# A threshold search on whole float32 scores, with a third tile counted by signs on ScalarE

## Chip, cores and metric

One core of one Trainium2 chip. The metric is the device time of one execution of the whole program in microseconds (us); the time before is the median of 3 runs.

## The reference, cut to what matters

The program is one step of a two-layer encoder trunk for 1024 prompt tokens and 32 sample tokens. The second layer's mixer is sparse attention: an indexer gives every query a score for every key, and each query attends to the 256 keys with the highest scores.

```
def dsa_attend_block(q, qi, wi, qpos, k, v, ki, kpos, topk):
    ...
    logits = jnp.einsum('bthd,bsd->bths', qi.astype(jnp.float32), ki.astype(jnp.float32)) * (IDX_DIM ** -0.5)
    score = jnp.einsum('bths,bth->bts', jax.nn.relu(logits), wi.astype(jnp.float32) * (IDX_HEADS ** -0.5))
    allowed = (kpos[None, :] // CHUNK) <= (qpos[:, None] // CHUNK)
    score = jnp.where(allowed[None], score, NEG)
    vals, idx = lax.top_k(score, topk)
    ...
```

## The kernel before, in words

The program runs in stages: the state-space layer, a feed-forward layer, the index scores, the projections of keys, values and queries, the attention, its output projection, and a second feed-forward layer. Residual and activations stay in SBUF; matrix products are made from exact high and low parts, three matmuls for each.

Tokens stand in nine tiles: 0 to 7 are 128 prompt tokens each, 8 is the sample's 32. Tile t may see `ext[t]` keys: 128 (t + 1) for the prompt, 1056 for the sample. Tiles 2 to 8 choose among more than 256 keys, and `index_scores` leaves their float32 scores in `sc[t]`, one row per query.

`select` (line 1063) finds the 256th highest score of each row, bit by bit, for all rows of all seven tiles at once. A step sets one bit of the candidate threshold, counts each row's scores that reach it, and keeps the bit where there are at least 256. VectorE counts tiles 7, 5, 4, 3 and 2 (`COMPS`) by a comparison with an accumulated output (line 1099); ScalarE counts tiles 8 and 6 (`SIGNS`) by the accumulated sign of score minus threshold (line 1102). Line 1105 compares the counts with 256 for all tiles (`up`), line 1111 sets the bit (`key`), line 1108 makes the next candidate, which both engines wait for. These three work on 2 to 7 columns; all such values lie in one tile, `small`.

The sign tiles are searched over whole float32 scores. The comparison tiles are searched over 16-bit halves: line 1080 copies the upper halves out as bfloat16 (`half`), 15 steps search those, then lines 1133 to 1141 count the scores above the found upper half and replace `half` by the lower halves of the scores that share it, and 16 steps search those as unsigned integers, with two more small operations in a step (lines 1146 and 1151).

The search is a generator. `project_heads` computes the projections in six jobs (keys, four groups of queries, values) of nine token tiles. A tile's product takes 24 matmuls (lines 772 to 774) into a PSUM bank, six of them in turn; ScalarE copies it out (line 1217) and after each copy `beside` lets 0.6 of a step of the search be recorded (`RATE`), on ScalarE behind that copy. So 54 copies and 31 steps share the engines, in the order in which a scheduler puts them on each queue; every queue is run in order. For keys and queries, three tiles at a time, ScalarE squares (line 1238), VectorE sums (line 1244), and GpSimd scales and rotates (lines 1247, 812 to 815, 1274). GpSimd also splits the weights (lines 140, 141).

`attend` follows. It takes the PSUM banks over once all copies are done, and reads keys, values and queries back from DRAM. `make_mask` turns a tile's threshold into a mask one step of `attend` ahead of its use: VectorE counts the scores above the threshold (line 1176); for a sign tile the key may be one too low, so three small operations raise it (lines 1181 to 1183) and line 1176 runs a second time; then lines 1185 to 1189 on VectorE and 1190, 1191 on GpSimd write the mask. On GpSimd's queue the split of the next queries (lines 1202, 1203) stands behind them, and PE's transposes of these (line 1336) wait for it.

Of the kernel before, what the change touches and what calls it, by code (L numbers as in the profile page):

```python
# [40 lines left out]
SIGNS, COMPS = [8, 6], [7, 5, 4, 3, 2]  # L41
# [8 lines left out]
class Trunk:  # L50
    """Shared tiles and helpers; the residual lives in xt[feature % 128, feature // 128, token]."""
# [13 lines left out]
    def open_dense(self, ctx):  # L65
        """The residual, from the first mixer's recurrence on."""
        self.main = ctx.enter_context(self.tc.tile_pool(name="main", bufs=1, reuse_waits="tile"))
        self.xt = self.main.tile([P, KD, T], F32, name="xt")

    def open_tables(self, ctx):  # L70
        """Constants of the second mixer."""
        nc, I = self.nc, self.I
        pool = ctx.enter_context(self.tc.tile_pool(name="tab", bufs=1, side="right", reuse_waits="tile"))
        self.tab = {}
        for nm in ("cos", "sin"):
            self.tab[nm] = pool.tile([P, 9, 16], F32, name=nm)
            nc.scalar.dma_start(self.tab[nm], I["c_" + nm])
# [17 lines left out]
    def load_vectors(self, pool):  # L95
        """Per-feature vectors, one column of 128 features each."""
# [34 lines left out]
    def weight(self, view, pool=False):  # L131
        """view [128, n] (rows on partitions): its two exact parts, as stationary operands; pool: split by the Pool engine."""
# [14 lines left out]
    def weight_rows(self, view, sh):  # L147
        """weight of a view whose rows lie apart."""
# [10 lines left out]
    def product(self, ps, terms):  # L159
        """ps += sum over (wh, wl, xh, xl) of w^T x, in float32 accuracy."""  # L160
# [8 lines left out]
    def rsqrt(self, y, m, tmp, iters=3):  # L169
        """y = m ** -0.5 elementwise; tmp: like y."""  # L170
# [68 lines left out]
    def store_block(self, pool, b):  # L239
        """y rows of block b."""  # L240
# [14 lines left out]
    def exp(self, pool, dst, x):  # L255
        """dst = exp(x) to float32 accuracy (range reduction, polynomial, exponent bits)."""
# [19 lines left out]
    def cmul(self, pool, orr, oi, xr, xi, yr, yi):  # L276
        """(orr + i oi) = (xr + i xi)(yr + i yi); shapes [.., s, n] already broadcast alike."""
# [44 lines left out]
    def ssm_params(self, pool, tmp, ld):  # L322
        """State-major tables of the discretized recurrence: partition = (re n | im n). The norm's gain is part of the inputs' taps."""
# [19 lines left out]
        # th = 2 pi k + (r + rl)  # L343
# [21 lines left out]
        # powers a^0 .. a^8  # L365
# [6 lines left out]
        # f = (a - 1) / lambda  # L372
# [22 lines left out]
        # rows to be transposed: 0-7 (Re af | Re af), 8-15 (-Im af | Im af), 16-23 (Re a | Re a),  # L395
        # 24-31 (-Im a | -Im a), 32 |a|^8, 33 state
# [24 lines left out]
        # turns per chunk of 8 tokens, in three parts  # L421
# [16 lines left out]
        # stationary rows (group | group): [0] parts 0 and 1, less a small shift; [1] part 0; [2] parts 1 and 2  # L438
# [13 lines left out]
        # input and output maps, state-major  # L452
# [63 lines left out]
        # the sample's rows take the place of b, c and the powers, which are of no more use  # L516
# [13 lines left out]
    def ssm(self):  # L530
        """xh + xl = gelu(S5(rmsnorm(x))), feature k*128 + g*16 + q at [q*8 + g, k]."""
        nc, I, O = self.nc, self.I, self.O
        C = 133  # chunk columns: 128 of the prompt, the sample's start state, 4 of the sample
        with ExitStack() as ctx:
# [34 lines left out]
            G0 = (0, 3, 6)  # groups are worked on three at a time  # L569
# [3 lines left out]
            def taps(o):  # L573
                """Input taps a^(7-j) f B, output taps C a^d, and |a|^8 of 8 groups."""
# [23 lines left out]
            def maps(o, d):  # L598
                """Within-chunk operands: inputs to state (re | im | re), inputs to outputs."""
# [25 lines left out]
            def angles(o, s):  # L625
                """cos and sin of the state's turns up to each chunk; the groups' inputs, [(j, cin), chunk]."""
# [31 lines left out]
            def states(d, w):  # L658
                """The states at the chunks' ends, turned back: the scan needs |a|^8 only; then their turned parts."""
# [38 lines left out]
            def rows(o):  # L698
                """Feature-major rows, gelu, parts in token order."""
# [34 lines left out]
            # final states  # L734
# [30 lines left out]
    def project(self, ps, t, w, kw, a, b):  # L765
        """ps[token, column] = xn[tokens of tile t] @ W[:, a:b], w: the parts of W's rows in pieces of kw k-tiles."""
# [9 lines left out]
    def open_spares(self):  # L776
        """Small tiles of the second mixer's first part, in the rooms of the norm's tiles."""
# [31 lines left out]
    def rotary(self, eng, r, x, cos, sin):  # L809
        """x[..., 0:16] rotated in place; cos, sin: tables broadcast to x[..., 0:16]; r: scratch like x[..., 0:16]."""  # L810
# [6 lines left out]
    def split_rows(self, hi, lo, ps):  # L817
        """Parts of ps: hi (all rows), lo."""
# [4 lines left out]
    def stack(self, dst, ps):  # L823
        """ps rows (x; x) -> dst rows (high part of x; low part of x)."""
# [4 lines left out]
    def attn_inputs(self, ctx):  # L829
        """Selection masks (in ctx's pool), and the projected heads, written to DRAM."""  # L830
# [18 lines left out]
        # the masks take the place of the scores  # L849
        mask = {i: sc[i].bitcast(BF)[:, : ext[i]] for i in sc}  # L850
        self.mask = mask
        with ExitStack() as pctx:
# [19 lines left out]
            def beside(ins):  # L872
                """Steps of the search, behind a copy of the projections."""
# [11 lines left out]
    def index_scores(self, ip, W, OQI, OKI, cos, sin, sc):  # L885
        """sc[i][q, key] = index scores of the query tiles that choose among more than 256 keys."""
# [11 lines left out]
        def keys(t, ps):  # L898
            """Keys of tile t rotated; returns the rest of the work."""
# [17 lines left out]
        def queries(t, ps, h0):  # L917
            """Four heads' queries of tile t rotated; returns the rest of the work."""
# [37 lines left out]
        # heads 4-7 with the keys and the weights of the heads, then heads 0-3  # L956
# [18 lines left out]
        # the sample: a sum over the heads by a product with their weights, four heads of the 32 queries and a fourth of  # L975
        # the keys (256 of the cache, 8 of its own) at a time; rows of the sum: (fourth, query)
# [3 lines left out]
        def sample_weights():  # L980
            """Weights as (head, query) x query, zeros around."""
# [79 lines left out]
    def select(self, mp, wk, sc):  # L1061
        """Thresholds: the 256th highest score of each row, bit by bit; make_mask does the rest. Scores that are counted by
        comparisons are searched by their upper, then by their lower halves, the others (counted by signs) as a whole."""
        nc = self.nc
        ext = self.ext
        BF, U16 = mybir.dt.bfloat16, mybir.dt.uint16
# [5 lines left out]
        rooms = [[wk.tile([P, T], F32, tag="kh", name="half").bitcast(BF), 2 * T]]  # L1072
        for tag in ("q", "q", "qi", "qi"):
            rooms.append([wk.tile([P, 512], F32, tag=tag, name="half", bufs=2).bitcast(BF), 1024])
        half = {}
        for t in sorted(COMPS, key=lambda t: -ext[t]):
            room = next(r for r in rooms if r[1] >= ext[t])
            room[1] -= ext[t]
            half[t] = room[0][: rows(t), room[1] : room[1] + ext[t]]
# [4 lines left out]
        sm = mp.tile([P, 13, n], F32, name="small")  # L1084
        d = {}
        for i, nm in enumerate(("cnt", "need", "thr", "a", "b", "low", "try", "key", "m", "cand", "up", "val", "x")):
            d[nm] = sm[:, i] if i < 7 else sm[:, i].bitcast(I32)
        cut = lambda v, i: v[: rows(ts[i]), i : i + 1]
        sg, cm = lambda v: v[:, 0:ns], lambda v: v[:, ns:n]
# [4 lines left out]
        def count(x, xs, op=ALU.is_ge, signs=None):  # L1094
            for i, t in enumerate(ts):
                o = cut(d["cnt"], i)
                if i >= ns:
                    turn[0] ^= 1
                    nc.vector.tensor_scalar(
                        junk[turn[0]][: rows(t), : ext[t]], xs[t], x if x == 0.0 else cut(x, i), 0.0, op0=op, op1=ALU.add, accum_out=o)  # L1100
                elif signs is not None:
                    nc.scalar.activation(junk[2][: rows(t), : ext[t]], sc[t][: rows(t)], AF.Sign, bias=signs if signs == 0.0 else cut(signs, i), accum_out=o)

        def reached():
            nc.vector.tensor_tensor(d["up"], d["cnt"], d["thr"], op=ALU.is_ge)

        def candidate(f, bit):
# [35 lines left out]
        for bit in range(15, -1, -1):  # L1143
            if ns:
                candidate(sg, bit)
# [584 lines left out]
```

## Time and profile before

| | us |
|---|---|
| median of 3 runs (lowest, highest) | 2805.51 (2801.63, 2806.05) |
| span of the profiled execution | 2799.6 |
| the median over that span | 5.9 |
| PE busy | 2582.2 (92%) |
| VectorE (DVE) busy | 1640.5 (59%) |
| ScalarE (ACT) busy | 976.6 (35%) |
| GpSimd (POOL) busy | 448.1 (16%) |

The profile gives one execution, taken by the hardware profiler; its time outside the span isn't given, so the span is its own time. PE's share is 92% over the whole, but the 40 slices of the profile dip for PE in the slices from 1390 us on, and VectorE's rise to nearly full: a stage with another limit. Times of rows are from the span's start.

### The profile page before, as it was taken

How to read it: one execution, taken by the hardware profiler on the slowest of the kernel's cores; microseconds unless marked ns; L12 is line 12 of the kernel's file. 1: busy time of each engine (PE TensorE's matmuls, PEld its weight loads, DVE VectorE, ACT ScalarE, POOL GpSimd, SP SyncE). 2: the span in 40 equal slices, each digit the busy share in tenths (PEclk: the TensorE clock that was granted, in tenths of full speed). 3: DMA queues.
4: the chain of work that ended last, by engine and by line, in shares of the span. 5: the costliest groups of instructions: out<-in, count | busy, mean ns of one | idle time of the engine just before them, and what ended most of it. 6: DMA issues, size and time to landing. Idle time of an engine off the chain costs nothing. (4 is left out here: it accounts for less than half of the span.)

```text
span 2799.6 us, 43287 instructions
## 1 busy us (share of the span) xinstructions
PE 2582.2 (92%) x17203; PEld 2473.0 (88%) x17203; DVE 1640.5 (59%) x3487; ACT 976.6 (35%) x1947; POOL 448.1 (16%) x696
## 2 busy tenths in 40 slices
PE   2887999999999999997986689999999999999999
PEld 2676999999999999996886667778999999999998
DVE  8886225644444444478799977663554444444443
ACT  4565213311111111134544466773331111111112
POOL 4672001100000000012144243220110000000000
PEclk9998999999999999998998889999999999999999
DMA  4334211111111111110121211212111111111111
GB/s 94 60 59 109 80 46 46 46 46 46 46 46 46 46 46 46 46 37 14 48 66 47 69 40 25 52 27 69 46 46 46 46 46 46 46 46 46 46 38 63
DMA packets 220662, 140.29 MB, mean 50 GB/s; under 512 B 50429, under 2 KB 212261, under 8 KB 220461
## 3 DMA queue, kind: packets, MB, share of 16 engines
q1 hardware_dynamic: 216733, 130.90, 17.0%
q10 hardware_dynamic: 3728, 6.64, 0.7%
q8 instruction: 135, 2.21, 0.3%
q14 instruction: 66, 0.54, 0.1%
HBM read 112.68 MB, written 13.40 MB: 45 GB/s over the span
## 5 line engine op out<-in xcount | busy, mean ns | idle before, releaser
L164 PE MATMUL ps_mm<-xh,whi 128*128 128x352 f32 x2688 | 870.4, 324 | 5.0 <-ACT whi L143 5.0
L166 PE MATMUL ps_mm<-xh,wlo 128*128 128x352 f32 x2688 | 869.6, 324 | 0.0
L165 PE MATMUL ps_mm<-xl,whi 128*128 128x352 f32 x2688 | 868.6, 323 | 0.0
L164 PEld LDWEIGHTS ps_mm<-xh,whi 128*128 128x128 f32 x2688 | 506.5, 188 | 5.3 <-ACT whi L143 5.2
L165 PEld LDWEIGHTS ps_mm<-xl,whi 128*128 128x128 f32 x2688 | 506.3, 188 | 0.0
L166 PEld LDWEIGHTS ps_mm<-xh,wlo 128*128 128x128 f32 x2688 | 506.0, 188 | 0.2 <-DVE wlo L144 0.2
L144 DVE TENSOR_TENSOR wlo<-wraw,whi 128x1024 fp32r<-128x1024 f32 (+1 forms) x145 | 175.5, 1222 | 416.4 <-ACT whi L143 416.4
L143 ACT CAST whi<-wraw 128x1024 fp32r<-128x1024 f32 (+1 forms) x145 | 149.9, 1047 | 712.1 <-PE ps_mm L165 702.3
L1603 DVE TENSOR_TENSOR xt<-xt,ps_mm 128x352 f32<-128x352 f32 x528 | 269.4, 520 | 191.5 <-PE ps_mm L166 191.4
L164 PE MATMUL ps_mm<-hh,whi 128*128 128x352 f32 x1056 | 341.0, 323 | 1.5 <-DVE xt L1603 1.5
L165 PE MATMUL ps_mm<-hl,whi 128*128 128x352 f32 x1056 | 340.9, 323 | 0.0
L166 PE MATMUL ps_mm<-hh,wlo 128*128 128x352 f32 x1056 | 340.7, 323 | 0.0
L1584 POOL COPY tails<-a 128x2 f32<-128x2 f32 x44 | 39.8, 904 | 1229.5 <-ACT a L1573 1229.5
L772 PE MATMUL ps_mm<-whi,xh 128*128 128x256 f32 (+3 forms) x560 | 165.8, 297 | 42.5 <-ACT raw L1217 42.5
L164 PEld LDWEIGHTS ps_mm<-hh,whi 128*128 128x128 f32 x1056 | 198.4, 188 | 2.1 <-DVE xt L1603 2.0
L166 PEld LDWEIGHTS ps_mm<-hh,wlo 128*128 128x128 f32 x1056 | 198.4, 188 | 0.0
L165 PEld LDWEIGHTS ps_mm<-hl,whi 128*128 128x128 f32 x1056 | 198.4, 188 | 0.0
L1591 DVE TENSOR_TENSOR c<-c,ps_mm 128x352 f32<-128x352 f32 (+2 forms) x176 | 71.5, 428 | 159.2 <-PE ps_mm L166 112.6
L774 PE MATMUL ps_mm<-whi,xl 128*128 128x256 f32 (+3 forms) x560 | 163.6, 293 | 0.0
L773 PE MATMUL ps_mm<-wlo,xh 128*128 128x256 f32 (+3 forms) x560 | 163.6, 293 | 0.0
L772 PEld LDWEIGHTS ps_mm<-whi,xh 128*128 128x128 f32 (+1 forms) x560 | 106.4, 190 | 47.4 <-ACT raw L1217 41.2
L1573 ACT COPY a<-ps_mm 128x352 f32<-128x352 f32 (+2 forms) x176 | 61.9, 378 | 242.1 <-PE ps_mm L166 242.0
(420 smaller groups left out, 3992.4 us busy)
## 6 DMA issues: line engine op xcount, KB each, us to landing
wraw<-in_ffn_w_up_dram SPq DMA_DIRECT2D x88, 512.0 KB
wraw<-in_ffn_w_down_dram SPq DMA_DIRECT2D x44, 512.0 KB
wraw<-in_ssm_w_glu_dram SPq DMA_DIRECT2D x128, 64.0 KB
wraw<-in_attn_w_in_dram SPq DMA_DIRECT2D x14, 512.0 KB
zo<-yo SPq DMA_DIRECT2D x64, 66.5 KB
xcm<-in_x_prompt_dram SPq DMA_DIRECT2D x8, 512.0 KB
cps<-cp SPq DMA_DIRECT2D x16, 256.0 KB
xrow<-in_x_prompt_dram ACTq DMA_DIRECT2D x8, 512.0 KB
```

The lines of the kernel that those rows point to most:

```text
L143: nc.scalar.copy(hi, raw)
L144: nc.vector.tensor_sub(lo, raw, hi.bitcast(F32))
L164: nc.tensor.matmul(ps, wh, xh, start=(i == 0), stop=False)
L165: nc.tensor.matmul(ps, wh, xl, start=False, stop=False)
L166: nc.tensor.matmul(ps, wl, xh, start=False, stop=(i == n - 1))
L772: self.nc.tensor.matmul(ps, xh, hi[:, c, a:b], start=(k == 0), stop=False)
L773: self.nc.tensor.matmul(ps, xh, lo[:, c, a:b], start=False, stop=False)
L774: self.nc.tensor.matmul(ps, xl, hi[:, c, a:b], start=False, stop=(k == KD - 1))
L1573: nc.scalar.copy(u["a"][:, co + 2 : co + 2 + n], ps[:, to - b * BLK : to - b * BLK + n])
L1584: nc.gpsimd.tensor_copy(tails[:, u["f"], 0:2], u["a"][:, TP : TP + 2])
L1591: nc.vector.tensor_mul(h, h, bv[:, to - b * BLK : to - b * BLK + n])
L1603: nc.vector.tensor_add(self.xt[:, m, blocks[b]], self.xt[:, m, blocks[b]], ps[:, :BLK])
```

## The change

All seven tiles are searched over whole float32 scores, in 31 alike steps (bits 30 to 0) after the first count. The copies of halves, the passage from upper to lower halves and the small operations of the lower steps are gone. Tile 2 moves from the comparisons to the signs, so VectorE counts four tiles a step and ScalarE three. (The change also drops comments, so the lines behind them have smaller numbers: line 1102 becomes 1089, 1099 becomes 1092, 1105 becomes 1093, 1111 becomes 1105, 1108 becomes 1103, 1217 becomes 1169, 1176 becomes 1128, 1190 becomes 1142, 1202 becomes 1154.)

```diff
-SIGNS, COMPS = [8, 6], [7, 5, 4, 3, 2]
+SIGNS, COMPS = [8, 6, 2], [7, 5, 4, 3]
...
-        half = {}
-        for t in sorted(COMPS, key=lambda t: -ext[t]):
...
-            nc.vector.tensor_copy(half[t], sc[t].bitcast(BF)[: rows(t), 1 : 2 * ext[t] : 2])
-        y = {t: half[t].bitcast(U16) for t in half}
...
-        def count(x, xs, op=ALU.is_ge, signs=None):
+        def count(x):
             for i, t in enumerate(ts):
-                o = cut(d["cnt"], i)
-                if i >= ns:
+                o, v = cut(d["cnt"], i), sc[t][: rows(t)]
+                c = x if x == 0.0 else cut(x, i)
+                if i < ns:
+                    nc.scalar.activation(junk[2][: rows(t), : ext[t]], v, AF.Sign, bias=c, accum_out=o)
+                else:
                     turn[0] ^= 1
-                    nc.vector.tensor_scalar(
-                        junk[turn[0]][: rows(t), : ext[t]], xs[t], x if x == 0.0 else cut(x, i), 0.0, op0=op, op1=ALU.add, accum_out=o)
...
+                    nc.vector.tensor_scalar(junk[turn[0]][: rows(t), : ext[t]], v, c, 0.0, op0=ALU.is_ge, op1=ALU.add, accum_out=o)
             nc.vector.tensor_tensor(d["up"], d["cnt"], d["thr"], op=ALU.is_ge)
...
-        for bit in range(30, 15, -1):
-            candidate(all_, bit)
-            count(cf, half, signs=cf)
-            reached()
-            settle(all_, bit)
-            yield
...
-        count(cf, half, ALU.is_gt)
...
-                nc.vector.tensor_scalar(half[t], half[t], cut(cf, i), cut(d["a"], i), op0=ALU.is_equal, op1=ALU.mult)
...
-        for bit in range(15, -1, -1):
...
-            nc.vector.tensor_scalar_add(cm(d["try"]), cm(d["low"]), float(1 << bit))
-            count(d["try"], y, signs=cf)
...
-            nc.vector.scalar_tensor_tensor(cm(d["low"]), cm(d["up"]), float(1 << bit), cm(d["low"]), op0=ALU.mult, op1=ALU.add)
+        for bit in range(30, -1, -1):
+            nc.vector.scalar_tensor_tensor(d["cand"], d["key"], 1 << bit, d["x"], op0=ALU.bitwise_or, op1=ALU.bitwise_xor)
+            count(d["cand"].bitcast(F32))
+            nc.vector.scalar_tensor_tensor(d["key"], d["up"], bit, d["key"], op0=ALU.logical_shift_left, op1=ALU.bitwise_or)
             if bit:
                 yield
```

VectorE at the last step of the search before and after (line 1099, now 1092, counts a tile; `small` holds the columns). Before:

```order
L1099 TENSOR_SCALAR junk,small<-half,small 128x1024
L1099 TENSOR_SCALAR junk,small<-half,small 128x768
L1099 TENSOR_SCALAR junk,small<-half,small 128x640
L1099 TENSOR_SCALAR junk,small<-half,small 128x512
L1099 TENSOR_SCALAR junk,small<-half,small 128x384
L1105 TENSOR_TENSOR small<-small 128x7
L1111 SCALAR_TENSOR_TENSOR small<-small 128x2
L1151 SCALAR_TENSOR_TENSOR small<-small 128x5
L1108 SCALAR_TENSOR_TENSOR small<-small 128x2
L1146 TENSOR_SCALAR small<-small 128x5
```

After:

```order
L1092 TENSOR_SCALAR junk,small<-score_11145,small 128x1024
L1092 TENSOR_SCALAR junk,small<-score_11143,small 128x768
L1092 TENSOR_SCALAR junk,small<-score_11142,small 128x640
L1092 TENSOR_SCALAR junk,small<-score_11141,small 128x512
L1093 TENSOR_TENSOR small<-small 128x7
L1105 SCALAR_TENSOR_TENSOR small<-small 128x7
L1103 SCALAR_TENSOR_TENSOR small<-small 128x7
```

A count and two small operations are gone, and the counts read the scores themselves.

ScalarE at the end of the projections, where the last step's signs stand among the last copies of values (`raw`) and their stores to DRAM (`vd`); `score_11146` is tile 8, `score_11144` tile 6, `score_11140` tile 2. Before:

```order
L1102 ACTIVATE junk,small<-score_11146,small 32x1056
L1102 ACTIVATE junk,small<-score_11144,small 128x896
L1217 COPY raw<-ps_mm 128x256
L1224 DMA vd<-raw 128x3x256
L1224 DMA out_v_prompt_dram<-raw 128x3x256
L1217 COPY raw<-ps_mm 128x256 x2
```

After:

```order
L1089 ACTIVATE junk,small<-score_11146,small 32x1056
L1089 ACTIVATE junk,small<-score_11144,small 128x896
L1169 COPY raw<-ps_mm 128x256
L1089 ACTIVATE junk,small<-score_11140,small 128x384
L1176 DMA vd<-raw 128x3x256
L1176 DMA out_v_prompt_dram<-raw 128x3x256
L1169 COPY raw<-ps_mm 128x256 x2
```

A third sign pass stands behind the other two, ahead of the last stores and copies; a copy can come between two passes.

GpSimd at the start of the attention, with tile 2's mask (`ms`, written to the place of `score_11140`) and the splits of queries (`qp`). Before:

```order
L1202 TENSOR_SCALAR qp<-qr 128x4x64
L1203 TENSOR_TENSOR qp<-qr,qp 128x4x64
L1190 TENSOR_TENSOR ms<-ms 128x384
L1191 TENSOR_SCALAR score_11140<-ms 128x384
L1202 TENSOR_SCALAR qp<-qr 128x4x64
L1203 TENSOR_TENSOR qp<-qr,qp 128x4x64
```

After:

```order
L1154 TENSOR_SCALAR qp<-qr 128x4x64
L1155 TENSOR_TENSOR qp<-qr,qp 128x4x64
L1142 TENSOR_TENSOR ms<-ms 128x384
L1154 TENSOR_SCALAR qp<-qr 128x4x64
L1143 TENSOR_SCALAR score_11140<-ms 128x384
L1155 TENSOR_TENSOR qp<-qr,qp 128x4x64
```

The second split still ends behind both operations of the mask.

## Rows read from the trace of the kernel before

**Rows 1.** Stretches of time: length, busy PE, PEld, DVE, ACT, POOL, clock, DMA.

```profile
1390.00:1604.00 214.00, 161.52 (x1279) 155.84 (x1278) 207.85 (x546) 102.10 (x199) 84.80 (x103) 0.91 0.17 53
```

**Rows 2.** Waits of 1390 to 1640 us: total us, times, longest.

```profile
PE ps_mm L772 <- ACT raw L1217: 42.5, 17, 13.0
...
PE ps_t L1324 <- ACT raw L1217: 9.0, 1, 9.0
```

**Rows 3.** DVE timeline, an upper step: start, us, engine, line, operation, [idle before].

```profile
1481.99 1.28 DVE L1099 TENSOR_SCALAR_CACHE_REDUCE junk<-half,small 128x1024 bf16<-128x1024 bf16 x1
...
1485.59 0.61 DVE L1099 TENSOR_SCALAR_CACHE_REDUCE junk<-half,small 128x384 bf16<-128x384 bf16 x1
1486.13 0.08 DVE L1099 DVE_READ_ACCUMULATOR junk<-half,small 128x1 f32 x1
1486.32 0.17 DVE L1105 TENSOR_TENSOR small<-small 128x7 int32<-128x7 f32 x1
1486.70 0.17 DVE L1111 SCALAR_TENSOR_TENSOR small<-small 128x7 int32<-128x7 int32 x1 [0.22 <-DVE small L1105]
...
1487.11 1.28 DVE L1099 TENSOR_SCALAR_CACHE_REDUCE junk<-half,small 128x1024 bf16<-128x1024 bf16 x1
```

**Rows 4.** DVE timeline, the passage between the halves.

```profile
1491.25 0.95 DVE L1244 TENSOR_REDUCE room<-sq 128x12 f32<-128x768 f32 x1
...
1493.01 0.17 DVE L1111 SCALAR_TENSOR_TENSOR small<-small 128x7 int32<-128x7 int32 x1
...
1509.46 1.27 DVE L1099 TENSOR_SCALAR_CACHE_REDUCE junk<-half,small 128x1024 bf16<-128x1024 uint16 x1
...
1510.66 0.61 DVE L1141 SCALAR_TENSOR_TENSOR half<-score,small,half 128x384 uint16<-128x384 uint16 x1
```

**Rows 5.** DVE timeline, a lower step, from its first count to the next one's.

```profile
1515.66 1.28 DVE L1099 TENSOR_SCALAR_CACHE_REDUCE junk<-half,small 128x1024 bf16<-128x1024 uint16 x1
...
1520.66 1.28 DVE L1099 TENSOR_SCALAR_CACHE_REDUCE junk<-half,small 128x1024 bf16<-128x1024 uint16 x1
```

**Rows 6.** DVE timeline, the last copy of halves, ahead of the first count.

```profile
1392.99 0.69 DVE L1080 COPY half<-score 128x1024 bf16<-128x1024 bf16 x1 [0.24 <-POOL score L1059]
```

**Rows 7.** Groups by shape: busy us, mean ns, idle before; search and masks.

```profile
L1099 DVE TENSOR_SCALAR_CACHE_REDUCE junk<-half,small 128x1024 bf16<-128x1024 bf16 x16 | 20.4, 1278 | 0.5
...
L1176 DVE TENSOR_SCALAR_CACHE_REDUCE ms<-score,small 128x1024 bf16<-128x1024 f32 x1 | 1.3, 1273 | 0.0
```

**Rows 8.** Groups by shape, the sign passes on ScalarE.

```profile
L1102 ACT ACTIVATE junk<-score,small 32x1056 bf16<-32x1056 f32 x31 | 36.4, 1176 | 107.3 <-DVE small L1108 79.5 <-DVE small L1146 27.8
L1102 ACT ACTIVATE junk<-score,small 128x896 bf16<-128x896 f32 x31 | 32.1, 1037 | 0.6
```

**Rows 9.** ACT timeline, a step's sign passes and copies, and a square.

```profile
1482.05 1.18 ACT L1102 ACTIVATE junk<-score,small 32x1056 bf16<-32x1056 f32 x1 [2.32 <-DVE small L1108]
...
1483.35 1.04 ACT L1102 ACTIVATE junk<-score,small 128x896 bf16<-128x896 f32 x1
...
1484.39 0.63 ACT L1217 COPY raw<-ps_mm 128x256 f32<-128x256 f32 x2
...
1488.34 0.83 ACT L1238 ACTIVATE sq<-raw 128x768 f32<-128x768 f32 x1
```

**Rows 10.** Timelines of DVE, POOL and PE, tile 2's mask.

```profile
1616.11 0.62 DVE L1189 SCALAR_TENSOR_TENSOR ms<-ms,small 128x384 bf16<-128x384 f32 x1
...
1616.86 0.91 POOL L1190 TENSOR_TENSOR ms<-ms 128x384 bf16<-128x384 bf16 x1 [6.52 <-ACT p L1362]
...
1619.72 0.75 PE L1336 MATMUL ps_t<-identr,qp 128*128 128x128 f32 x4 [4.21 <-POOL qp L1203]
```

**Rows 11.** DVE timeline, the raising of a sign tile's key (tile 6).

```profile
1670.97 0.14 DVE L1181 TENSOR_SCALAR small<-small 128x1 int32<-128x1 f32 x1
...
1672.34 1.15 DVE L1176 TENSOR_SCALAR_CACHE_REDUCE ms<-score,small 128x896 bf16<-128x896 f32 x1
```

**Rows 12.** Groups of the search's stretch, DVE: busy us, mean ns.

```profile
L1108 DVE SCALAR_TENSOR_TENSOR small<-small 128x2 int32<-128x2 int32 (+1 forms) x31 | 11.2, 360 | 0.4
```

More of the change, by code (lines that the diff above doesn't have):

```diff
@@ L1065, in select @@
         ext = self.ext
-        BF, U16 = mybir.dt.bfloat16, mybir.dt.uint16
+        BF = mybir.dt.bfloat16
         K = 256.0
@@ L1071, in select @@
         rows = lambda t: self.toks[t][1]
-        rooms = [[wk.tile([P, T], F32, tag="kh", name="half").bitcast(BF), 2 * T]]
-        for tag in ("q", "q", "qi", "qi"):
-            rooms.append([wk.tile([P, 512], F32, tag=tag, name="half", bufs=2).bitcast(BF), 1024])
-        half = {}
-        for t in sorted(COMPS, key=lambda t: -ext[t]):
-            room = next(r for r in rooms if r[1] >= ext[t])
-            room[1] -= ext[t]
-            half[t] = room[0][: rows(t), room[1] : room[1] + ext[t]]
-            nc.vector.tensor_copy(half[t], sc[t].bitcast(BF)[: rows(t), 1 : 2 * ext[t] : 2])
-        y = {t: half[t].bitcast(U16) for t in half}
         junk = [wk.tile([P, T], BF, tag="r", name="junk", bufs=3) for _ in range(3)]
         turn = [0]
-        sm = mp.tile([P, 13, n], F32, name="small")
+        sm = mp.tile([P, 9, n], F32, name="small")
         d = {}
-        for i, nm in enumerate(("cnt", "need", "thr", "a", "b", "low", "try", "key", "m", "cand", "up", "val", "x")):
-            d[nm] = sm[:, i] if i < 7 else sm[:, i].bitcast(I32)
+        for i, nm in enumerate(("cnt", "need", "thr", "key", "m", "cand", "up", "val", "x")):
+            d[nm] = sm[:, i] if i < 3 else sm[:, i].bitcast(I32)
         cut = lambda v, i: v[: rows(ts[i]), i : i + 1]
-        sg, cm = lambda v: v[:, 0:ns], lambda v: v[:, ns:n]
         nc.vector.memset(d["cnt"], 0.0)
@@ L1092, in select @@
             nc.vector.memset(d["thr"][:, i : i + 1], 2 * K - ext[t] if i < ns else K)
-        def count(x, xs, op=ALU.is_ge, signs=None):
+        def count(x):
             for i, t in enumerate(ts):
-                o = cut(d["cnt"], i)
-                if i >= ns:
-                    turn[0] ^= 1
-                    nc.vector.tensor_scalar(
-                        junk[turn[0]][: rows(t), : ext[t]], xs[t], x if x == 0.0 else cut(x, i), 0.0, op0=op, op1=ALU.add, accum_out=o)
-                elif signs is not None:
-                    nc.scalar.activation(junk[2][: rows(t), : ext[t]], sc[t][: rows(t)], AF.Sign, bias=signs if signs == 0.0 else cut(signs, i), accum_out=o)
-        def reached():
-            nc.vector.tensor_tensor(d["up"], d["cnt"], d["thr"], op=ALU.is_ge)
-        def candidate(f, bit):
-            nc.vector.scalar_tensor_tensor(f(d["cand"]), f(d["key"]), 1 << bit, f(d["x"]), op0=ALU.bitwise_or, op1=ALU.bitwise_xor)
-        def settle(f, bit):
-            nc.vector.scalar_tensor_tensor(f(d["key"]), f(d["up"]), bit, f(d["key"]), op0=ALU.logical_shift_left, op1=ALU.bitwise_or)
-        all_ = lambda v: v
-        count(0.0, half, signs=0.0)
-        reached()
+                o, v = cut(d["cnt"], i), sc[t][: rows(t)]
[3 more added lines that the diff above has]
+                else:
+                    turn[0] ^= 1
+                    nc.vector.tensor_scalar(junk[turn[0]][: rows(t), : ext[t]], v, c, 0.0, op0=ALU.is_ge, op1=ALU.add, accum_out=o)
+            nc.vector.tensor_tensor(d["up"], d["cnt"], d["thr"], op=ALU.is_ge)
+        count(0.0)
         nc.vector.tensor_single_scalar(d["key"], d["up"], 31, op=ALU.logical_shift_left)
@@ L1118, in select @@
         nc.vector.tensor_single_scalar(d["m"], d["m"], TOP, op=ALU.bitwise_or)
+        nc.vector.tensor_copy(d["x"], d["m"])
         if ns:
-            nc.vector.tensor_single_scalar(sg(d["x"]), sg(d["m"]), TOP, op=ALU.bitwise_xor)
-        nc.vector.tensor_copy(cm(d["x"]), cm(d["m"]))
-        nc.vector.tensor_scalar(d["a"], d["up"], 2.0, -1.0, op0=ALU.mult, op1=ALU.add)
-        nc.vector.tensor_scalar(d["b"], d["up"], 65535.0, -65535.0, op0=ALU.mult, op1=ALU.add)
-        cf = d["cand"].bitcast(F32)
@@ L1126, in select @@
-        for bit in range(30, 15, -1):
-            candidate(all_, bit)
-            count(cf, half, signs=cf)
-            reached()
-            settle(all_, bit)
-            yield
-        nc.vector.tensor_tensor(cm(d["cand"]), cm(d["key"]), cm(d["m"]), op=ALU.bitwise_xor)
-        nc.vector.tensor_single_scalar(cm(d["cand"]), cm(d["cand"]), -65536, op=ALU.bitwise_and)
-        count(cf, half, ALU.is_gt)
-        nc.vector.tensor_scalar(cm(d["thr"]), cm(d["cnt"]), -1.0, K, op0=ALU.mult, op1=ALU.add)
@@ L1137, in select @@
-        nc.vector.memset(d["low"], 0.0)
-        for i, t in enumerate(ts):
-            if i >= ns:
-                nc.vector.tensor_scalar(half[t], half[t], cut(cf, i), cut(d["a"], i), op0=ALU.is_equal, op1=ALU.mult)
-                nc.vector.scalar_tensor_tensor(
-                    y[t], sc[t].bitcast(U16)[: rows(t), 0 : 2 * ext[t] : 2], cut(d["b"], i), half[t], op0=ALU.add, op1=ALU.mult)
-        for bit in range(15, -1, -1):
-            if ns:
-                candidate(sg, bit)
-            nc.vector.tensor_scalar_add(cm(d["try"]), cm(d["low"]), float(1 << bit))
-            count(d["try"], y, signs=cf)
-            reached()
-            if ns:
-                settle(sg, bit)
-            nc.vector.scalar_tensor_tensor(cm(d["low"]), cm(d["up"]), float(1 << bit), cm(d["low"]), op0=ALU.mult, op1=ALU.add)
+            nc.vector.tensor_single_scalar(d["x"][:, 0:ns], d["m"][:, 0:ns], TOP, op=ALU.bitwise_xor)
```

2 lines of the change are left out of this document (removed).

## The prediction

> **What bounds the kernel now.** Over the whole program PE is the busiest, so the view to read first is the one of busy time by stretches, to see whether the change lies where PE is the limit. It doesn't. In the 214 us of the projections, in which the search runs, VectorE is busy 207.85 us, PE 161.52, ScalarE 102.10, GpSimd 84.80 [rows 1]. Next, the waits of that stretch, to see who is held up by whom: PE waits 42.5 us in 17 places for ScalarE's copies out of PSUM, and then 9.0 us, at the change to the attention, for the last of them [rows 2]. Those copies are not slow; they stand in ScalarE's queue behind sign passes, and the sign passes wait 107.3 us for the next candidate from VectorE, at line 1108 in the upper and the lower steps and at line 1146, which the queue puts last in a lower step [rows 8]. So the chain is: VectorE counts, makes the candidate, ScalarE may run its signs and then its copies, a PSUM bank comes free, PE goes on. VectorE's queue is the limit of this stage, and what is saved there until the candidate of the last step comes forward at the end of the stage. The timeline of VectorE then gives the pieces of a step.
>
> **A step.** In the upper step shown, four counts (1024, 768, 640, 512 columns) take from 1481.99 to 1485.59, that is 3.60 us; the fifth, of tile 2, takes 0.54 more until the next instruction; 0.19 us later comes line 1105, and the next step's first count starts at 1487.11 [rows 3]. The step is 5.12 us, of which 0.22 was idle ahead of line 1111 [rows 3]; I leave that piece out, so 4.90.
>
> **What goes, on VectorE, up to the last candidate.**
> 1. Tile 2's count in the first round and in the 30 steps ahead of the last: 31 x 0.54 = 16.7 us.
> 2. The passage between the halves. Without it the step would go from line 1111 at 1493.01 to a first count 0.41 us later (1487.11 - 1486.70 [rows 3]), at 1493.42. It came at 1509.46 [rows 4], so 16.0 us, with a whole further round of counts among it. One operation of the passage, line 1141 on tile 2, stands behind that count and takes 0.5 us more: 16.5.
> 3. The further small operations of the lower steps: 5.00 us a step [rows 5] against 4.90, 15 times, 1.5 us.
> 4. The last copy of halves, 0.69 us straight ahead of the first count [rows 6]: 0.7. The other four copies stand earlier, among the index scores, and none is wider; I count nothing for them, and at most 4 x 0.69 = 2.8 us in the range.
>
> Together 35.4 us.
>
> **What the counts cost on whole scores.** The search's trace has no float32 count, but the masks do: line 1176 is the same instruction with float32 in and bfloat16 out. It takes 1273 ns for 1024 columns, where the 16-bit count takes 1278 [rows 7]. The price is the same, so this edit costs 0. The Trainium skill ("VectorE: DVE Perf Modes", the perf-mode tier table) gives one-source operations four elements a cycle for bfloat16 in SBUF and two for float32, which speaks against the change: by it a whole score would count at half the rate of a half. The rows above contradict it for this operation, 1278 ns against 1273; the time that it would give is a rival below.
>
> **What comes.** ScalarE gets a third pass in every round. No row has a sign pass of 384 columns. Between 1056 and 896 columns the passes differ by 139 ns [rows 8], 0.87 ns a column, so 384 columns come to 1037 - 512 x 0.87, some 590 ns. From below the bound is 0, from above that of the 896 columns, 1.04; I take 0.59, as the two rows lie on a line. Does it lengthen the step? From candidate to the end of the three passes it is 0.1 + 1.30 + 1.04 + 0.59, and 0.1 for the accumulator, 3.1 us [rows 9], against 3.60 + 0.19 on VectorE [rows 3]. In the new order a copy (0.35 at most) stands between the passes in 19 of 32 rounds, a square (0.83) as well in four of these: 3.5 and 4.3 us. In the latter VectorE has the sum of that square in the same step, 0.95 us [rows 4], so 4.6. ScalarE stays ahead, by 0.3 us where it is closest, and its cover is VectorE's own queue. The new pass is on the path once, ahead of the last copies: 0.6 us.
>
> PE has room: it could give up at most its 42.5 us of waits [rows 2], more than the 35 of VectorE. So VectorE still sets the stage, with PE waiting some 7 us there and the 9 us at the switch as before. GpSimd has the same work in fewer us: 84.80 of 214 becomes 84.80 of some 179. That matters through the small operations: line 1108 takes 0.17 us when undisturbed, and 360 ns in the mean, 11.2 us in all [rows 12], 5.9 above its due. Lines 1105 and 1111 are of the same kind. Such time may grow with GpSimd's share or fall with the operations gone; I leave it as it is and keep 9 us either way for the range.
>
> In the attention tile 2 is now a sign tile, so its mask needs lines 1181 to 1183 and a second count. For tile 6 the three small operations took from 1670.97 to 1672.34, 1.37 us, some of them drawn out [rows 11]; undisturbed they would take 0.2 each. With 0.54 for the count that is 1.1 to 1.9 us; I take 1.4. It isn't hidden: VectorE's last piece of tile 2's mask ends at 1616.73, GpSimd takes it at 1616.86, the queries' split stands behind it in GpSimd's queue, and PE's transposes wait 4.21 us for that until 1619.72 [rows 10]. ScalarE released GpSimd at about the same moment, so nearly all of it counts. The moved line 1191 saves nothing, for the split's second half still stands behind it. No DMA is added or taken away.
>
> **The sum.** 35.4 - 0.6 - 1.4 = 33.4 us. The profiled span was 2799.6 us and would be 2766.2; the median of the runs lies 5.9 us above that span, so 2772 us is my forecast. Chance 0.83. Its own range is 2762 to 2784: downwards the 9 us of small operations and part of the 2.8 of the copies of halves; upwards 9 us again, 0.5 for the mask's upper bound, and some 2.3 for a sign pass at its upper bound, 0.45 us dearer, in the four rounds with a square and the last.
>
> **The rivals.**
> - ScalarE becomes the limit of the step. Against it is the margin above; for it, that the margin is 0.3 us in some rounds and copies that wait for PE would stand ahead of the next signs. If the third pass came on the path in each of the 31 rounds, it would take back 31 x 0.59 = 18 us: a gain of 15, 2790 us. It decides once the passes end later than 3.8 us behind the candidate. Chance 0.08.
> - Whole-score counts run at twice the rate of today's. The float32 count of rows 7 speaks against it. Then VectorE is no limit, and PE's waits are the bound of the gain: 42.5 us go, 0.6 and 1.4 come, and some 2 us of the 9.0 at the switch may go as well [rows 2]: 2763 us. Chance 0.04.
> - Whole-score counts run at half that rate, and the program gets slower. Each of 32 rounds then costs 3.60 us more, 115 us, against 35 saved: 80 more, and the two small terms, 2887 us. It decides from a count that is 31% dearer (35.4 / 115) on. The 1273 ns of the masks' count speak against it [rows 7]. Chance 0.03. This is the time that the table of the Trainium skill's page named above would give, if it held for this operation.
> - The end of the stage doesn't move, since something else than the copies holds the attention back. PE's waits for exactly these copies speak against it: 2805 us. Chance 0.02.
>
> **How the numbers follow.** A measurement of this kernel tells 0.2%, 5.6 us, from no change; so faster means below 2799.9. The first three cases are that, 0.95; the last is within, 0.02; slower 0.03. The range takes in the forecast's own, the edge of the doubled rate and the nearer part of ScalarE's case: 2762 to 2787.
>
> **What would show it.** Right: 1273 ns for a count of 1024 whole scores; steps of some 4.4 us, 5.1 with a sum of squares; a stage of projections of some 179 us in place of 214; PE's wait for copies near 7 us; the third sign pass at 0.6 us. ScalarE's rival would show as idle time of line 1093 until a sign pass. Wrong: counts at another price, or a line 1103 (the old 1108) that takes much more than 11 us in all.

## The result, and the profile after

The changed kernel takes 2777.4 us (median of 4 runs, 2774.8 to 2782.5), the kernel before 2805.8 (median of 4). The ratio is 0.9907, 95% interval 0.9895 to 0.9919: 26 us faster, between 23 and 29 (the medians alone lie 28.4 us apart). 33.4 were forecast. The two profiled executions show less of it, 2799.6 - 2780.7 = 18.9 us: that of before was the quickest of its runs, that of after the slowest.

The stage first. Busy time of the changed kernel up to the attention (columns as in [rows 1]):

```profile
1390.00:1580.00 190.00, 157.75 (x1307) 152.56 (x1305) 182.55 (x427) 125.73 (x267) 83.70 (x103) 0.97 0.19 60
```

VectorE is still the limit, 182.55 of 190 us. PE's waits in and behind the stage (total, number, longest):

```profile
PE ps_mm L772 <- ACT raw L1169: 25.1, 16, 2.9
...
PE ps_t L1276 <- ACT raw L1169: 6.2, 1, 6.2
```

Of the 42.5 us of waits for copies [rows 2] 25.1 are left, where some 7 were forecast; the wait at the switch to the attention fell from 9.0 to 6.2. The search on VectorE, from its first count to the last round's first count, before:

```profile
1393.72 1.22 DVE L1099 TENSOR_SCALAR_CACHE_REDUCE junk<-half 128x1024 bf16<-128x1024 bf16 x1
...
1598.33 1.28 DVE L1099 TENSOR_SCALAR_CACHE_REDUCE junk<-half,small 128x1024 bf16<-128x1024 uint16 x1
```

and after:

```profile
1395.13 1.22 DVE L1092 TENSOR_SCALAR_CACHE_REDUCE junk<-score 128x1024 bf16<-128x1024 f32 x1 [0.43 <-POOL score L1059]
...
1574.41 1.28 DVE L1092 TENSOR_SCALAR_CACHE_REDUCE junk<-score,small 128x1024 bf16<-128x1024 f32 x1
```

204.6 us became 179.3. With the 0.7 us of the last copy of halves [rows 6] VectorE gained 26.0 us up to that point, where the forecast had 35.4. PE's first transposes of the attention came forward by 23.8 (shown further below): the first count itself stands 1.4 us later in this execution, and in the runs of this document it stands anywhere from 1390.9 to 1396.1 us. The groups of VectorE in the stage show where 9.4 us stayed. After (busy us, mean ns, idle before):

```profile
L1092 DVE TENSOR_SCALAR_CACHE_REDUCE junk<-score,small 128x1024 bf16<-128x1024 f32 x31 | 39.6, 1279 | 1.0
...
L1105 DVE SCALAR_TENSOR_TENSOR small<-small 128x7 int32<-128x7 int32 x31 | 13.7, 441 | 1.1 <-DVE small L1093 0.2
L1093 DVE TENSOR_TENSOR small<-small 128x7 int32<-128x7 f32 x32 | 13.0, 407 | 1.9
...
L1103 DVE SCALAR_TENSOR_TENSOR small<-small 128x7 int32<-128x7 int32 x31 | 11.0, 356 | 0.9
```

Before, their like beside line 1108 [rows 12]:

```profile
L1111 DVE SCALAR_TENSOR_TENSOR small<-small 128x2 int32<-128x2 int32 (+1 forms) x31 | 8.6, 276 | 1.1 <-DVE small L1105 0.2
L1105 DVE TENSOR_TENSOR small<-small 128x7 int32<-128x7 f32 x32 | 7.7, 242 | 1.8
```

Counts cost what was forecast (1279 ns against 1278). The three small operations of a step, 94 in either kernel, went from 11.2 + 8.6 + 7.7 = 27.5 us to 37.7. VectorE isn't waiting for ScalarE: line 1093 has 1.9 us of idle time ahead of it in all 32 rounds. A round's end, on VectorE:

```profile
1495.01 0.19 DVE L1093 TENSOR_TENSOR small<-small 128x7 int32<-128x7 f32 x1
1495.23 0.32 DVE L1105 SCALAR_TENSOR_TENSOR small<-small 128x7 int32<-128x7 int32 x1
1495.58 2.32 DVE L1103 SCALAR_TENSOR_TENSOR small<-small 128x7 int32<-128x7 int32 x1
1497.94 1.28 DVE L1092 TENSOR_SCALAR_CACHE_REDUCE junk<-score,small 128x1024 bf16<-128x1024 f32 x1
```

and GpSimd at the same time:

```profile
1495.13 0.39 POOL L813 TENSOR_TENSOR room<-raw,room 128x96 f32<-128x96 f32 x1
1495.48 2.40 POOL L141 TENSOR_TENSOR wlo<-wraw,whi 128x1024 fp32r<-128x1024 f32 x1
1497.84 1.43 POOL L1199 TENSOR_TENSOR raw<-raw,room 128x576 f32<-128x576 f32 x1
```

Line 1105 ends when line 813 does, line 1103 (seven columns, 2.32 us) when line 141 does. The count that follows runs beside line 1199 in its usual 1.28 us. In this trace 31 of the 94 small operations are longer than 0.27 us, before 14; each of the long ones ends within 0.04 us of an operation of GpSimd. The converse holds too: of the 94, 31 began while an operation of GpSimd that reads SBUF had at least 0.25 us to go, in the kernel before 14, and every one of these took 0.27 us or more. Those that met no such operation took at most 0.172 us in both kernels.

### The profile page after: what moved, and what is told of

The parts are those of the page before. It is cut to its first block, busy times and chain, and to the rows that moved or that the text cites. A ratio compares the mean times of both kernels' runs of the same rounds, so it can differ in the third digit from the quotient of the medians.

```text
span 2780.7 us, 43227 instructions
## 1 busy us (share of the span) xinstructions
PE 2579.9 (93%) x17203; PEld 2470.6 (89%) x17203; DVE 1612.4 (58%) x3363; ACT 997.7 (36%) x2011; POOL 446.2 (16%) x696
## 5 line engine op out<-in xcount | busy, mean ns | idle before, releaser
L772 PE MATMUL ps_mm<-whi,xh 128*128 128x256 f32 (+3 forms) x560 | 162.7, 291 | 25.2 <-ACT raw L1169 25.1
L772 PEld LDWEIGHTS ps_mm<-whi,xh 128*128 128x128 f32 (+1 forms) x560 | 104.1, 186 | 29.7 <-ACT raw L1169 28.6
```

Of the source, the lines that this page charges most:

```text
L772: self.nc.tensor.matmul(ps, xh, hi[:, c, a:b], start=(k == 0), stop=False)
```

## The experiments

**Theory A:** a small operation of VectorE waits for GpSimd's running operation because it reads two operands from SBUF; the changed kernel packs the same work of GpSimd into a shorter search, so more of them meet it, and that took the missing part. **Theory B:** ScalarE's third pass holds the steps up. Each ratio below is to runs of the kernel before made together with the experiment's; their medians were 2802.4 to 2803.8 us, where 2805.8 stood beside the changed kernel, so absolute times shift by 2 to 3 us for that reason alone.

**1. Whole scores alone.**

```diff
-SIGNS, COMPS = [8, 6, 2], [7, 5, 4, 3]
+SIGNS, COMPS = [8, 6], [7, 5, 4, 3, 2]
```

> The changed kernel with tile 2 counted on VectorE again (two sign tiles, five counted tiles): only the change to whole scores is left. By the terms of the prediction this part is worth 16.0 + 0.5 + 1.5 + 0.7 = 18.7 us, so 2787. Theory A (VectorE's small operations wait for GpSimd operations more often once the steps are denser): part of that is lost here already, 2788 to 2796, and lines 1093, 1105 and 1103 together take more than the 27.5 us that their like took before. Theory B (ScalarE's third pass holds up the steps): nothing is lost here, 2787, and the small operations stay near 27.5 us.

Measured: 2786.5 us, ratio 0.9944 (0.9932 to 0.9957), 15.7 us faster than before. The time can't decide: as a gain, theory A had 9.5 to 17.5 us and theory B 18.5, and the interval is 12 to 19 (as an absolute time 2786.5 even lies at theory B's 2787). The small operations decide, 32.0 us against 27.5 before, as theory A had it; the forecast's 18.7 less 4.5 is 14.2.

```profile
L1093 DVE TENSOR_TENSOR small<-small 128x7 int32<-128x7 f32 x32 | 11.3, 354 | 1.9
L1103 DVE SCALAR_TENSOR_TENSOR small<-small 128x7 int32<-128x7 int32 x31 | 11.2, 361 | 0.9
L1105 DVE SCALAR_TENSOR_TENSOR small<-small 128x7 int32<-128x7 int32 x31 | 9.5, 306 | 0.8
```

**2. The third sign tile alone,** on the kernel before.

```diff
-SIGNS, COMPS = [8, 6], [7, 5, 4, 3, 2]
+SIGNS, COMPS = [8, 6, 2], [7, 5, 4, 3]
```

> The kernel before, with tile 2 moved to ScalarE's sign passes and the 16-bit halves kept: only the third sign tile is left. By the terms of the prediction: 32 counts of 0.54 us and the 0.5 us of line 1141 on tile 2, less 0.6 and 1.4 us, 15.8 us, so 2790. Theory A: something is lost, the more GpSimd operations meet the small ones: 2791 to 2797. Theory B: ScalarE takes back up to 18 us, so 2795 or more, and VectorE stands idle ahead of line 1105 until sign passes end.

Measured: 2792.6 us, ratio 0.9966 (0.9952 to 0.9979), 9.5 us faster: the two parts add up to the whole, 25.2 and 26. The time fits both theories; the groups don't. From 1390 to 1600 us VectorE has two waits, 2.8 us, neither for a sign pass: 0.2 us for a score ahead of the search, 2.6 in the attention behind it. The small operations are dear again (32.4 us), among them line 1146, 7.6 us where it took 3.4 before:

```profile
L1105 DVE TENSOR_TENSOR small<-small 128x7 int32<-128x7 f32 x32 | 11.2, 349 | 1.8
L1111 DVE SCALAR_TENSOR_TENSOR small<-small 128x3 int32<-128x3 int32 (+1 forms) x31 | 10.9, 351 | 0.9
L1108 DVE SCALAR_TENSOR_TENSOR small<-small 128x3 int32<-128x3 int32 (+1 forms) x31 | 10.3, 333 | 0.4
L1146 DVE TENSOR_SCALAR small<-small 128x4 f32<-128x4 f32 x15 | 7.6, 508 | 0.0
```

**3 and 4. Thresholds and keys in PSUM,** so that each of the three small operations has at most one input in SBUF, in the changed kernel:

```diff
+        keep = dict(d)
+        pt = self.ps("aux")[:, : 2 * n].rearrange("p (a n) -> p a n", n=n)
+        for i, nm in enumerate(("thr", "key")):
+            d[nm] = pt[:, i] if i < 1 else pt[:, i].bitcast(I32)
...
+        nc.vector.tensor_copy(keep["key"], d["key"])
+        d = keep
```

> The changed kernel with the search's thresholds and keys in PSUM, so that each of the three small operations of a step has one of its two inputs outside SBUF. Nothing else is changed. Theory A: the 21.8 us that lines 1093, 1105 and 1103 take above 0.17 us apiece (37.8 us of 94) go, less at most some 0.05 us for each of 94 operations on PSUM: 2756 to 2761, the small operations together at 16 to 21 us. If the operations wait for something else than a second input in SBUF: no change, 2777, small operations at 38 us. If PE is the limit by then: 2761 to 2770, with the small operations short all the same and VectorE idle.

and in the kernel before, with `low` as a third such value:

> The kernel before with thresholds, keys and the lower halves' bounds in PSUM, in the same way. Theory A: it loses only its own stalls, 27.5 - 94 x 0.17 = 11.5 us (and some 2 of lines 1146 and 1151), less at most 4.7: 2792 to 2799. The difference between this kernel and the changed one with its state in PSUM is then what the change is worth without stalls: 33 to 38 us by theory A, about 28 by theory B, where ScalarE took the rest.

Measured: 2756.3 us, ratio 0.9835 (0.9822 to 0.9849), for the changed kernel, and 2789.9, ratio 0.9954 (0.9941 to 0.9966), for the one before (2 us under the range expected). The changed kernel with its state in PSUM, groups of VectorE:

```profile
L1109 DVE SCALAR_TENSOR_TENSOR ps_aux<-small,ps_aux 128x7 int32<-128x7 int32 x31 | 5.3, 169 | 0.9
L1097 DVE TENSOR_TENSOR small<-small,ps_aux 128x7 int32<-128x7 f32 x32 | 5.1, 160 | 1.9
L1107 DVE SCALAR_TENSOR_TENSOR small<-ps_aux,small 128x7 int32<-128x7 int32 x31 | 5.1, 165 | 0.9
L173 DVE TENSOR_SCALAR room<-room 128x12 int32<-128x12 int32 x3 | 4.9, 1643 | 0.1
```

A round's end in it, on VectorE:

```profile
1484.65 0.15 DVE L1097 TENSOR_TENSOR small<-small,ps_aux 128x7 int32<-128x7 f32 x1
1484.84 0.17 DVE L1109 SCALAR_TENSOR_TENSOR ps_aux<-small,ps_aux 128x7 int32<-128x7 int32 x1
1485.05 0.17 DVE L1107 SCALAR_TENSOR_TENSOR small<-ps_aux,small 128x7 int32<-128x7 int32 x1
1485.25 1.28 DVE L1096 TENSOR_SCALAR_CACHE_REDUCE junk<-score,small 128x1024 bf16<-128x1024 f32 x1
```

beside GpSimd:

```profile
1484.51 0.61 POOL L814 TENSOR_TENSOR raw<-raw,room 128x192 f32<-128x192 f32 x1
1485.19 0.60 POOL L815 TENSOR_TENSOR raw<-raw,room 128x192 f32<-128x192 f32 x1
```

GpSimd's line 814 runs beneath all three, and none is long. Nor are there fewer meetings: 37 of the 94 began while such an operation of GpSimd had at least 0.25 us to go (31 in the changed kernel), and the longest of the 94 took 0.171 us. The small operations fell from 37.7 us to 15.5, by 22.2; the time fell by 21.1 (20.2 by the ratios). PE's waits for copies went from 25.1 to 7.5 us, as VectorE comes forward:

```profile
PE ps_mm L772 <- ACT raw L1175: 7.5, 9, 2.7
```

In the kernel before, they fell from 27.5 us to 15.3, and the time by 13.1. Between the two kernels without these stalls lie 33.6 us (33.4 by the ratios), as much as the forecast's sum had for the change. Theory A holds, and B, by which about 28 would have been left, doesn't: even the slowest run of the one (2758.9) and the quickest of the other (2787.4) lie 28.6 apart.

**5. No third sign pass** (`continue` for tile 2 in the loop over the sign tiles; tile 2's threshold is not searched then, and its values are set to zero).

> The changed kernel without ScalarE's pass over tile 2, whose threshold is then not searched (its three state values are set to zero after the search). Theory A (ScalarE's third pass is hidden but for its last time): 0.6 us faster, within 4 us of 2777, since the phase of GpSimd's operations may shift too. Theory B (the third pass holds the steps up): 8 to 18 us faster, 2759 to 2769, with less idle time of VectorE ahead of line 1093.

Measured: 2774.1 us, ratio 0.9900 (0.9886 to 0.9914), 3.3 us less than the changed kernel. Its small operations took 32.7 us, 5.0 less, so the pass's own price can't be told from that shift; the 8 us or more of theory B it is not.

**6. Only the comparison's outcome in PSUM.**

```diff
+        keep = dict(d)
+        d["up"] = self.ps("aux")[:, :n].bitcast(I32)
...
+        d = keep
```

> The changed kernel with only the outcome of the comparison in PSUM. Line 1093 then reads two operands from SBUF and writes PSUM, line 1105 reads one from PSUM and one from SBUF, line 1103 reads two from SBUF. If two inputs in SBUF are what makes an operation wait for GpSimd: line 1105 is short always (5.3 us in all), lines 1093 and 1103 still have long ones, over 9 us each. If any operand in PSUM, also the output, is enough: line 1093 is short as well. By either theory the time lies between 2756 and 2777.

Measured: 2773.1 us, ratio 0.9894 (0.9880 to 0.9907). Here line 1095 is the comparison, 1107 the key, 1105 the candidate:

```profile
L1105 DVE SCALAR_TENSOR_TENSOR small<-small 128x7 int32<-128x7 int32 x31 | 13.9, 450 | 0.9
L1095 DVE TENSOR_TENSOR ps_aux<-small 128x7 int32<-128x7 f32 x32 | 13.6, 424 | 1.9
...
L1107 DVE SCALAR_TENSOR_TENSOR small<-ps_aux,small 128x7 int32<-128x7 int32 x31 | 5.1, 165 | 1.1 <-DVE ps_aux L1095 0.2
```

The output's place doesn't matter; the second input from SBUF does. And a mended operation hands its wait to the next one: the key lost 8.6 us, the candidate took up 2.9 of them.

**7 and 8. Other phases:** the rate of steps to a copy is 0.62, in the kernel before and in the changed one.

```diff
-RATE = 0.6
+RATE = 0.62
```

> The kernel before with the search's steps issued at a rate of 0.62 to a copy in place of 0.6, so that its steps meet GpSimd's operations at other phases. If the small stall of the kernel before (27.5 us in its 94 small operations, where only 1 of 8 of line 141's 2.4 us operations met a small one) was luck of its order: 30 us or more, several meetings with line 141, 2805 to 2815. If it goes with the density of the work alone: 25 to 30 us, and 2801 to 2807.

> The changed kernel with the rate of 0.62. If the stalls go with the density of GpSimd's work alone: 34 to 41 us in the 94 small operations, 2773 to 2781. If luck of the order is the larger part: they may lie anywhere between 28 and 41 us, and the time moves with them, by as many us.

Measured: 2806.9 us, ratio 1.0013 (1.0004 to 1.0023), and 2775.8, ratio 0.9902 (0.9889 to 0.9916). GpSimd is busy for 83.5 to 85.4 us between the first and the last small operation of each of these kernels, so the length of that stretch stands for its density:

| kernel | stretch, us | 94 small operations, us |
|---|---|---|
| before, rate 0.62 | 208.0 | 27.4 |
| before | 205.1 | 27.5 |
| signs alone | 192.6 | 32.4 |
| whole scores alone | 189.0 | 32.0 |
| changed | 179.7 | 37.7 |
| changed, rate 0.62 | 176.3 | 34.6 |
| changed, no third pass | 176.2 | 32.7 |

The small stall of the kernel before was no luck of its one order: the other gives 27.4. Denser searches stall more, 12 us above the 15.5 of undisturbed operations in the longest, 17 to 22 in the shortest. The order decides over some 5 us among the shortest. Why the stall grows more steeply than the density isn't settled.

**9 and 10. From the version in PSUM on:** tiles 7 and 6 exchanged (`SIGNS, COMPS = [8, 7, 2], [6, 5, 4, 3]`), and the rate of 0.62.

> The changed kernel with its state in PSUM (2756.3 us) and the tiles 7 and 6 exchanged: ScalarE counts 8, 7 and 2, VectorE 6, 5, 4 and 3. VectorE's round loses 1273 - 1140 ns (128 columns at some 1.04 ns), 4 us in 31 rounds; ScalarE's grows by 0.11 us. If VectorE still sets the pace: 2752 to 2753. If PE or ScalarE do by now: no gain, 2755 to 2758.

> The changed kernel with its state in PSUM, steps issued at a rate of 0.62. There are no stalls left for the phase to change, so the time moves only by the wait at the switch to the attention (5.1 us with 0.6): 2751 to 2757, and the small operations stay at 15 to 16 us.

Measured: 2754.1 us, ratio 0.9823 (0.9809 to 0.9836), between the two ranges expected, and 2758.0, ratio 0.9840 (0.9827 to 0.9854), 1 us above its range. Neither can be told from 0.9835. The exchange saves VectorE 115.3 - 110.3 = 5.0 us of counts; its search is 3.4 us shorter, 155.1 against 158.5 from the first count to the last round's first. Whether that reaches the end these runs can't tell. At the rate of 0.62 the small operations stayed at 15.5 us.

**11. The keys' roots too.** The one row above of the PSUM version that doesn't fit two inputs is line 173: one input, 1643 ns. Two of its three took 2.43 and 2.33 us, each beside GpSimd's line 141 with 2.40. One of the two, on VectorE and on GpSimd:

```profile
1415.61 2.43 DVE L173 TENSOR_SCALAR room<-room 128x12 int32<-128x12 int32 x1
...
1415.61 2.40 POOL L141 TENSOR_TENSOR wlo<-wraw,whi 128x1024 fp32r<-128x1024 f32 x1
```

The edit, beside a place in PSUM for the next operation's output:

```diff
...
+                    if a == 0:
+                        pk = self.ps("aux")[:, 0:72]
+                    mk, uk = pk[:, 4 * a : 4 * a + 12], pk[:, 36 + 4 * a : 48 + 4 * a]
-                    nc.vector.tensor_scalar(s, s, 1.0 / 64.0, EPS, op0=ALU.mult, op1=ALU.add)
+                    nc.vector.tensor_scalar(mk, s, 1.0 / 64.0, EPS, op0=ALU.mult, op1=ALU.add)
...
```

> The changed kernel with its state in PSUM, and with the first three operations of the keys' roots (the scaling, lines 173 and 174) with their input or output in PSUM as well; each has one input only. In the run before this one, line 173, one input, both sides in SBUF, took 1643 ns in the mean of 3, beside GpSimd. If a plain operation with one input waits for GpSimd only where both its sides are in SBUF: the three take some 0.17 us each, and the wait moves to the next operation with two inputs in SBUF (line 176) or vanishes; 2752 to 2757. If one-input operations wait wherever their operands are: some of the three are still over 1 us, and the time is that of the kernel without this edit, 2756.

Measured: 2751.2 us, ratio 0.9810 (0.9797 to 0.9823), the fastest of all, 53 us under the kernel before; its interval just touches that of 0.9835. Lines 173, 174 and 176 are now 174, 175 and 177:

```profile
L177 DVE TENSOR_TENSOR room<-room 128x12 f32<-128x12 f32 x9 | 3.5, 392 | 0.1
...
L174 DVE TENSOR_SCALAR ps_aux<-ps_aux 128x12 int32<-128x12 int32 x3 | 0.5, 179 | 0.1
L1234 DVE TENSOR_SCALAR ps_aux<-room 128x12 f32<-128x12 f32 x3 | 0.5, 174 | 0.1
L175 DVE TENSOR_SCALAR room<-ps_aux 128x12 int32<-128x12 int32 x3 | 0.5, 171 | 0.0
```

The three are short, and the wait moved to line 177, the next with two inputs in SBUF, where it is smaller (3.5 us of 9 against 1.5 before this edit).

## Why the prediction was right, and which term failed

The direction, the bound and the mechanism held: VectorE sets the stage, and what it is spared comes out at PE. The time, 2777.4, lies 5 us above the forecast, inside the range; the 9 us that the range kept for the small operations are about what they took, and no row gave that number. Point by point:

1. **Whole scores cost what halves did:** 1279 ns against 1278 for 1024 columns. The perf-mode tier table of the Trainium skill ("VectorE: DVE Perf Modes"), which gives float32 half the rate of bfloat16, doesn't hold for this form of the operation, with an accumulated output.
2. **Tile 2's counts, the passage and the last copy of halves** are gone: without the stalls of the small operations the two kernels differ by 33.6 us, forecast 33.4. That the sums agree so closely is luck in part. In the profiled executions of those two, which lie 31.3 us apart, the search is 32.7 us shorter (191.2 and 158.5) where 34.7 were forecast; the 16.0 us of the passage had been read with two stalls in them, line 1133 with 2.25 us and line 1136 with 1.42. The attention gave back 3.6 (320.0 and 323.6) where 1.4 were forecast; the rest lies at the stage's two ends.
3. **The third sign pass** takes 615 ns (0.59 was estimated), and VectorE doesn't wait for ScalarE. The 0.6 us that the pass was to cost once, ahead of the last copies, doesn't show: from the last round's first count to PE's transposes it is 2.72 us before and 2.80 after, since the copy that these wait for (at 1576.81) stands ahead of the pass (at 1577.07).

```profile
L1089 ACT ACTIVATE junk<-score,small 128x384 bf16<-128x384 f32 x31 | 19.1, 615 | 0.5
```

4. **The term that failed** is the one on the small operations: "such time may grow with GpSimd's share or fall with the operations gone; I leave it as it is". It grew, by 10.2 us in 94 operations, and that covers the 9.4 that VectorE's search fell short by. The prediction saw the stalls and that GpSimd's share would rise from 84.80 of 214 us to the same of some 179, but gave them 9 us either way and a middle of nothing. There was no reason for the other way: no small operation left the upper steps. Nor would its own sign of being wrong have told: that was a line 1103 much above 11 us, and line 1103 took 11.0. The growth went to lines 1093 (7.7 to 13.0) and 1105 (8.6 to 13.7), which the prediction calls "of the same kind". The trace of before shows already that such an operation takes what is left of GpSimd's; on VectorE and on GpSimd:

```profile
1416.01 1.33 DVE L1108 SCALAR_TENSOR_TENSOR small<-small 128x7 int32<-128x7 int32 x1
...
1415.85 1.48 POOL L1274 TENSOR_TENSOR raw<-raw,room 128x768 f32<-128x768 f32 x1 [10.53 <-DVE small L1105]
```

They end together. The Trainium skill ("SBUF — State Buffer", Who interferes with whom) gives a reason. By it VectorE and GpSimd share a pair of SBUF ports, which the one that comes first holds for a whole instruction; VectorE wants it for two inputs in SBUF, against an operation of GpSimd that reads SBUF, and for plain one-input operations in a two-port mode, but not for the form with an accumulated output nor with at most one input in SBUF outside those modes. The runs here agree: counts 1278 and 1279 ns in the two kernels, small operations 407 ns with two inputs in SBUF and 160 with one, line 173 1643 ns in SBUF and, as line 174, 179 in PSUM.
5. **The mask of tile 2** was put at 1.4 us. PE's wait for the queries grew from 4.21 us [rows 10] to 5.23, 1.0:

```profile
1596.86 0.75 PE L1288 MATMUL ps_t<-identr,qp 128*128 128x128 f32 x4 [5.23 <-POOL qp L1155]
```

But the attention as a whole gives back more. From PE's first transposes to its first matmul behind the attention, before:

```profile
1601.05 1.97 PE L1324 MATMUL ps_t<-ident,kr 128*128 128x128 f32 x8 [9.02 <-ACT raw L1217]
...
1919.73 0.66 PE L164 MATMUL ps_mm<-xh,whi 128*128 128x352 f32 x1 [4.96 <-ACT whi L143]
```

and after:

```profile
1577.21 1.97 PE L1276 MATMUL ps_t<-ident,kr 128*128 128x128 f32 x8 [6.24 <-ACT raw L1169]
...
1900.78 0.66 PE L164 MATMUL ps_mm<-xh,whi 128*128 128x352 f32 x1 [5.16 <-ACT whi L143]
```

318.7 us became 323.6. With the rate of 0.62 it is 317.6 and 319.0, and with whole scores alone, without the new mask, 318.8. So the attention gives back 1.4 us at one rate and 4.9 at the other, of which 1.0 is the wait for the new mask. The rest of the 4.9 goes with PE's clock. Busy time from the transposes to that matmul, before and after (columns as in [rows 1]):

```profile
1601.05:1919.73 318.68, 286.62 (x2597) 229.50 (x2597) 222.55 (x769) 225.88 (x556) 92.56 (x158) 0.95 0.17 42
...
1577.21:1900.78 323.57, 290.43 (x2597) 233.02 (x2597) 222.49 (x769) 226.38 (x558) 92.22 (x158) 0.93 0.16 41
```

The same 2597 matmuls kept PE busy 3.8 us longer at a granted clock of 0.93 in place of 0.95; with the rate of 0.62 and with whole scores alone it is 0.95 as before, in experiment 3 (attention 323.6 us) 0.93. In the changed kernel the granted clock is 0.50, the level of 1.2 GHz, from 1643 to 1649 us and again from 1658 to 1661. Why it falls there in some of the runs stays open.
6. **The rivals.** ScalarE as the limit is excluded by experiments 2 to 5; half and double rate by the counts' 1279 ns; the end of the stage moved, by 23.8 us at PE's transposes.

## What to carry to other kernels

Work of another engine that a change leaves as it was becomes denser when the stage is shortened, and what stalls on it grows; give such a term a sign, not only a width. Where VectorE's smallest operations are drawn out, lay them beside GpSimd's timeline: if they end together, moving one of two inputs to PSUM takes the stall away, here some 21 us for six lines. Do it for all operations of the chain, for the wait goes on to the next exposed one.

## What was not expected of the hardware

An operation on seven columns took up to 2.32 us in the changed kernel with both inputs in SBUF. With one of them in PSUM, 500 of 501 small operations in six runs took at most 0.172 us, and one 0.34, behind a stalled line 173 (experiment 9); PSUM itself cost nothing that shows (160 to 169 ns in the mean). Only GpSimd's operations with an input seem to count: line 1105 ran at 1479.97 us of the changed kernel in 0.17 us, inside a memset of GpSimd's (1479.85, 0.31 us), right behind a line 1093 of 0.38 us that ended with line 815. A one-input operation on 12 columns stalled as well when both its sides lay in SBUF (1643 ns in the mean), and not with one side in PSUM (171 to 179), while counts over 1024 columns of SBUF, which accumulate, were never touched (1279 ns in the mean, the longest of any run 1.284 us).
